# The joint inside the first FFN: band exchange moved from a load to the stores, and another order for the first pair's sums of quarters

## The chip, the core and the metric

The kernel runs on one core of one Trainium2 chip. The metric is device time in microseconds (us) of one execution. Three timed executions of the kernel before gave 2583.55, 2589.14 and 2589.63 us; the median is 2589.14 us.

The engines are named as the profile names them: PE is TensorE (matmuls), PEld its weight loads, DVE is VectorE, ACT is ScalarE, POOL is GpSimd, SP is SyncE, which here only issues transfers. Transfers issued by SP go to the hardware queue that the profile calls q1; transfers issued by POOL, which here add what they read to what already stands in the destination, go to the software queue q0. Both queues are served by the same 16 DMA engines.

## The reference

One layer of a hybrid backbone over 256 latent and 256 context tokens with a model width of 2048: a gated FFN, a mixer (attention and a matrix LSTM side by side), a second gated FFN, a final norm. The change touches only the first FFN, which is done for both sequences, 512 tokens together:

```python
def adaln(x, g, mod, i):
    return rms_norm(x, g) * (1 + mod[:, i + 1, None, :]) + mod[:, i, None, :]

def half_step_ffn(x, mod, i, g, w_up, w_down):
    h = adaln(x, g, mod, i)
    a, b = jnp.split(h @ w_up, 2, axis=-1)
    return x + 0.5 * mod[:, i + 2, None, :] * ((jax.nn.silu(a) * b) @ w_down)
```

`D_FF` is 5632. Everything is float32.

## The kernel before, in words

**Precision.** A float32 operand is kept as two parts, `hi` (rounded) and `lo` (the rest), and a product is three matmuls: hi·hi, lo·hi, hi·lo (`mm3`, L154). The parts of a weight tile are made by `split`: for each half of a 128x2048 tile ACT writes `hi` (L130) and DVE subtracts to get `lo` (L131). There are four buffers for `hi` halves and four for `lo` halves, so the splitting can run about two tiles ahead of PE.

**The gated part, "quads".** The 5632 hidden columns are handled in 11 blocks of 512 (`FB` = 4 columns of 128). Block 0 is made near the start. Blocks 1 to 10 are made by `quad(n)`, each with seven block products instead of eight (a Strassen-like scheme over quarters of tokens and inner dimension). A quad has 14 steps: seven products `m`, two weight tiles `q` each, step number 2m+q. A step is 24 matmuls of 128x512. Some weight tiles are sums of tiles; the sums are made by adding transfers from POOL into a tile that was already used (`accum`, L742), into the two `chain` tiles or into a `raw` tile. At each step the quad also does one item of the modulation products (`mod_items`, loads `sraw` at L239, DVE work at L210).

**Storing a gated block.** A finished quarter of the block (tokens by hidden columns, `ca`) is transposed by DVE in 32x32 squares (L842, in `turned`) and stored to DRAM (L844) as it is. A transposition in 32x32 squares leaves bands of 32 rows in the wrong place. The exchange of these bands is done when the block is loaded again: `hid_load` for n > 0 issues four transfers (L713), each of which gathers rows of 512 B. Block 0 is stored in its final layout and is loaded by one plain transfer (L709).

**The down part, "pairs".** `pair(p)`, p from 0 to 4, multiplies two blocks (2p and 2p+1) with their part of `w_down`, again by seven products (`a11 a12 n1 s4 s2 s3 a22`) of two steps each, 14 steps of 24 matmuls. Each block stands in a tile `raws[0]` or `raws[1]` of 1 MB, which the trace calls `hidh` and `hidl` after the slots they take over. `raws[0]` holds the quarters a11 and a21, `raws[1]` holds a12 and a22. The seven moving operands are sums and differences of these quarters, made in place: v = a22 - a21; n1 = v; v2 = -v - a11 (this is s2); u turns a12 into s4; u2 turns a21 into a11 - a21 (this is s3). DVE makes the differences (L1020, L1021), and `split_to` (ACT L722, DVE L723) puts each operand's hi and lo parts into its place in `sums` (`sumshh` holds a11 a12 n1 s4, `sumshl` holds s2 s3 a22). The first pair takes a11 and a12 from two extra places (`place0`), which are filled in steps 11 and 12 of the last quad. PE's results are copied into `acc` by ACT (L1092) or added to it by DVE (L1094).

**The joint.** In the last quad (`last_steps`) the two blocks of the first pair are loaded at steps 6 and 8. In the first pair everything that a later pair does ahead of time still has to be done. What is done at which step is written in a table, `first_plan` (L1049): each step's words are carried out after that step's weight tile was split. `raw0` and `raw1` there are the loads of the next pair's two blocks (`hid_load` 2 and 3) into the same two places, which is possible once all sums from the place have been made.

**Order of instructions.** The program text gives a priority; a planner with its own estimate of durations makes a fixed list for each engine and queue from it. So an instruction may stand in its engine's list a little earlier or later than its text, and at run time each engine and SP's queue follow their list strictly.

Of the kernel before, what the change touches and what calls it, by code (L numbers as in the profile page):

```python
# [9 lines left out]
F32 = mybir.dt.float32  # L10
# [9 lines left out]
P = 128  # L20
# [8 lines left out]
NF = D_FF // P  # L29
# [18 lines left out]
FB = 4  # L48
CB = 512
# [11 lines left out]
def tile_layer(ctx: ExitStack, tc: tile.TileContext, I: dict, out: bass.AP):  # L61
    nc = tc.nc
# [7 lines left out]
    dr = ctx.enter_context(pool(name="dr", bufs=1, space=DRAM))  # L70
# [4 lines left out]
    def bank():  # L75
        return ps["mm"].tile([P, 512], F32, tag="mm", name="mm")

    def tbank():
        return ps["tr"].tile([P, 512], F32, tag="tr", name="tr")
# [189 lines left out]
    class Beside:  # L269
# [26 lines left out]
        def one(self):  # L296
            i, kt, h = self.items[self.n]
            x, limit = self.slots[self.n]
            mod_half(x, {LAT: self.cB}, None, i, (LAT,), kt, h)
            self.due.append((self.done + 1, self.n))  # L300
            self.n += 1
# [162 lines left out]
    with pool(name="st", bufs=1) as st:  # L464
# [53 lines left out]
        def factor(ss4):  # L518
            s1 = sm.tile([P, 1], F32, tag="s1", name="s1")
            vector[0].tensor_reduce(s1, ss4, axis=AX.X, op=ALU.add)  # L520
            r = sm.tile([P, 16], F32, tag="rstd", name="rstd", bufs=4)[:, :1]
            vector[0].tensor_scalar(r, s1, 1.0 / D, EPS, op0=ALU.mult, op1=ALU.add)
            nc.gpsimd.tensor_tensor(r, r, mhalf[:, :1], op=ALU.pow)
            return r
# [34 lines left out]
        def mod_unit():  # L559
            if ready:  # L560
                return ready.pop(0)
            raw = st.tile([P, 2048], F32, tag="mraw", name="mraw", bufs=4)
            tc.keep_in_program_order(nc.sync.dma_start(raw, I["w_m0"][next(unit)]))
            return raw
# [40 lines left out]
        for s in (CTX, LAT):  # L605
            for t in range(2):
                x = xs0[s, t] = st.tile([P, D], F32, name=f"xs{s}{t}")
# [20 lines left out]
        r = factor(ss)  # L628
        for n, (s, t) in enumerate(((CTX, 1), (LAT, 0), (LAT, 1))):
# [5 lines left out]
            last, r = r, factor(ss)  # L635
# [14 lines left out]
        for k0, k1 in BLOCKS[1:]:  # L650
            kk = slice(k0, k1)
            following = products(1, pre, k0, k1, hhi, hlo, middle=True)
            if k1 - k0 == 2:
                raw = mod_unit()
# [38 lines left out]
        vector[0], tensor[0] = nc.vector, nc.tensor  # L693


    hidd = [dr.tile([4, P, CB] if n else [P, 16, P], F32, name=f"hid{n}") for n in range(NF // FB)]
    NB = NF // FB
    fmcm = pool(name="fm", bufs=1, side="right")
    fm = fmcm.__enter__()
# [3 lines left out]
    def form(tag, name):  # L703
        sp = ft if tag == "t" else fm
        return [sp.tile([P, 2, 8, P], F32R, tag=f"{tag}{x}", name=f"{name}{x}") for x in "hl"]

    def hid_load(n, raw):
        if not n:
            nc.sync.dma_start(raw, hidd[0].rearrange("p m x -> p (m x)"))  # L709
            return  # L710
        rows = hidd[n].rearrange("m (a r) (b x) -> b r (m a) x", a=4, b=4)
        for b in range(4):
            nc.sync.dma_start(raw[32 * b : 32 * b + 32].rearrange("r (m x) -> r m x", x=P), rows[b])  # L713

    def pinned(ins):
        tc.keep_in_program_order(ins)
# [26 lines left out]
    with pool(name="f1u", bufs=1) as f1u:  # L743
# [28 lines left out]
        for f in range(NPRE, FB):  # L772
            pab = []
            for ab in range(2):
                wt = load_split(I["w_up1"][f - NPRE, ab])
                b = bank()
# [6 lines left out]
        n1, s2, s4 = form("n", "n1"), form("s", "s2"), form("t", "s4")  # L783
# [3 lines left out]
        a11, a12, a21, a22 = quarter(0, 0), quarter(0, 1), quarter(1, 0), quarter(1, 1)  # L787
        s3 = a21
# [46 lines left out]
        def turned():  # L835

            if not turn:
                return
            n, t, ca, spare = turn.pop(0)
            if (n, t) == (NB - 1, 3):  # L840
                spare = chp.tile([P, CB], F32, tag="stg", name="stg")
            pinned(nc.vector.transpose(spare, ca))  # L842
            s, tt = divmod(t, 2)
            nc.sync.dma_start(hidd[n][2 * tt + s], spare)  # L844

        add = lambda o, x, y: nc.vector.tensor_tensor(o, x, y, op=ALU.add)
        negative = lambda o, y: nc.vector.scalar_tensor_tensor(o, o, -1.0, y, op0=ALU.mult, op1=ALU.mult)
# [4 lines left out]
        def quad(n, after=lambda step: None):  # L852
# [84 lines left out]
            for m, (a, src, dst, fresh, then, use) in enumerate(order):  # L937
                if fresh:
                    dst.update({s: bank() for s in range(2)})
                for q in range(2):  # L940
                    wt = split(src(q))
                    if then:
                        then(q)
                    after(2 * m + q)
                    for s in range(2):
                        for j in range(4):
                            k = 4 * q + j
                            hi, lo = a[0][:, s, k, :], a[1][:, s, k, :]
                            mm3(dst[s], hi, lo, *wt(slice(j * CB, (j + 1) * CB)), fresh and k == 0, k == 7, True)
                        if q and use:  # L950
                            use(s)
                        elif not s:
                            turned()
# [20 lines left out]
        def last_steps(step):  # L974

            if step not in (6, 7, 8, 9):
                steps(side)
            if step == 6:
                raws.extend(hid_slot("n"))
            if step in (6, 8):  # L980
                hid_load(step // 2 - 3, raws[step // 2 - 3].bitcast(F32))
            if step == 10:
                place0.extend(x.rearrange("p (a c) -> p a c", a=2) for x in hid_slot("s"))
            if step in (11, 12):
                split_to(place0[step - 11], quarters(raws[step - 11].bitcast(F32))[0])
# [7 lines left out]
        while turn:  # L993
            turned()
# [51 lines left out]
        "last1": lambda: last_split(1),  # L1046
    }

    first_plan = {0: "v n1", 1: "v2 u s4", 2: "s2 u2", 3: "s3 a22", 4: "raw0 raw1", 7: "a11", 8: "a12", 9: "v n1", 10: "v2 u", 11: "s4", 12: "s2 u2", 13: "s3"}  # L1049
    plan = {0: "a22 raw0", 1: "raw1", 4: "a11", 5: "a12", 6: "v", 7: "n1", 8: "v2 u", 9: "s4", 11: "s2 u2", 13: "s3"}  # L1050
    last_plan = {0: "a22 raw0", 4: "last0", 5: "last1"}

# [24 lines left out]
    def pair(p):  # L1077
# [80 lines left out]
        for m, (g, src, dst, fresh, then, use) in enumerate(order):  # L1158
            a = place0[m] if p == 0 and m < 2 else place[g]
            for c in range(2):  # L1160
                wt = split(src(c))
                if then:
                    then(c)
                added()
                for x in todo.get(2 * m + c, "").split():
                    if x.startswith("raw"):
                        hid_load(2 * p + 2 + int(x[3]), raws[int(x[3])])
                    else:
                        make[x]()
                if p == NP - 1:  # L1170
                    if (2 * m + c) in GATES:
                        ahead.append(both_gates(GATES[2 * m + c]))
                    if 2 * m + c == 13:
                        last_gate(0)
                        last_gate(1)
                    if m in (1, 4, 6):
                        gates = used[c] = ahead.pop(0)
                    elif m == 5:
                        gates = used[c]
                for s in range(2):  # L1180
                    if fresh:
                        dst[c, s] = tbank() if c and dst is not X else bank()
                    for j in range(FB):
                        k = slice((2 * j + s) * P, (2 * j + s + 1) * P)
                        mm3(dst[c, s], a[:, 0, k], a[:, 1, k], *wt(slice(j * CB, (j + 1) * CB)), fresh and j == 0, j == FB - 1, True)
                    use(c, s)
# [92 lines left out]
    with ExitStack() as mx:  # L1279
# [47 lines left out]
        u = one([P, 4, 2, NH], "u")  # L1327
# [149 lines left out]
        for h in range(NH):  # L1477
            b = bank()
# [82 lines left out]
        for h in range(NH):  # L1561
            b = bank()[:, :T]
# [389 lines left out]
    with f2x:  # L1952
# [28 lines left out]
        for f in range(NPRE, FB):  # L1981
            pab = []
            for ab in range(2):
                wt = load_split(I["w_up2"][f - NPRE, ab])
                b = (tbank() if f == FB - 1 else bank())[:, :T]
# [33 lines left out]
        a11, a12, a21, a22 = quarter(0, 0), quarter(0, 1), quarter(1, 0), quarter(1, 1)  # L2019
        forms2 = {g: f3.tile([P, 2, 8, P], F32R, tag=f"f{i}", name=f"{g}f") for i, g in enumerate(("n1", "s4", "s2", "s3"))}  # L2020
        n1, s4, s2, s3 = ([x[:, 0], x[:, 1]] for x in (forms2[g] for g in ("n1", "s4", "s2", "s3")))
# [263 lines left out]
        for x in sequence():  # L2285
            next(streams[x])
            if x == "u":
                steps(forms)
            clock[0] += 1
            turned()  # L2290
# [164 lines left out]
```

## Time and profile before

| What | Value |
|---|---|
| median of three timed executions | 2589.14 us |
| profiled execution, its own time | 2593.71 us |
| span of the profiled execution | 2592.0 us |
| PE busy | 2557.9 us (99%) |
| DVE busy | 2223.8 us (86%) |
| ACT busy | 1403.2 us (54%) |
| the first FFN's last quad, from step 10 on | from 899.88 us |
| the first pair's first matmul | 924.93 us |

Times in the trace are counted from the start of the span. A row of the timeline has the start, the duration, the engine, the line of the kernel, the operation, the tiles written and read, and in square brackets how long the engine had been idle before and what ended that. Rows marked SPq are transfers being issued; their duration is the time SP spent on issuing. A row of the table by stretches gives, for each engine, busy time and number of instructions, then the granted clock of PE (1.00 is full), the share of the DMA engines' time and GB/s.

### The profile page before, as it was taken

How to read it: one execution, taken by the hardware profiler on the slowest of the kernel's cores; microseconds unless marked ns; L12 is line 12 of the kernel's file. 1: busy time of each engine (PE TensorE's matmuls, PEld its weight loads, DVE VectorE, ACT ScalarE, POOL GpSimd, SP SyncE). 2: the span in 40 equal slices, each digit the busy share in tenths (PEclk: the TensorE clock that was granted, in tenths of full speed). 3: DMA queues.
4: the chain of work that ended last, by engine and by line, in shares of the span. 5: the costliest groups of instructions: out<-in, count | busy, mean ns of one | idle time of the engine just before them, and what ended most of it. 6: DMA issues, size and time to landing. Idle time of an engine off the chain costs nothing. (4 is left out here: it accounts for less than half of the span.)

```text
span 2592.0 us, 33866 instructions
## 1 busy us (share of the span) xinstructions
PE 2557.9 (99%) x12486; PEld 2123.5 (82%) x12486; DVE 2223.8 (86%) x2942; ACT 1403.2 (54%) x1798; POOL 213.8 (8%) x262
## 2 busy tenths in 40 slices
PE   8999999999999999999999999999999999999998
PEld 5788888888887878888889889888898888888886
DVE  7789889888888878888887889898889888898887
ACT  5454444444444455444454347466476676666663
POOL 0000000000000000010110000120000000000001
PEclk8999999999999999999999999999999999999999
DMA  9988999999999999999987887776768999999986
GB/s 392 353 215 260 267 269 268 240 272 270 274 263 271 239 233 237 224 215 232 231 243 265 305 304 249 239 272 220 265 238 241 274 275 277 282 283 274 272 250 169
DMA packets 152182, 675.26 MB, mean 261 GB/s; under 512 B 22728, under 2 KB 43720, under 8 KB 91856
## 3 DMA queue, kind: packets, MB, share of 16 engines
q1 hardware_dynamic: 123936, 490.64, 51.7%
q0 software_dynamic: 28080, 182.46, 35.7%
q8 instruction: 98, 1.61, 0.2%
q14 instruction: 68, 0.56, 0.1%
HBM read 655.15 MB, written 17.89 MB: 260 GB/s over the span
## 5 line engine op out<-in xcount | busy, mean ns | idle before, releaser
L130 ACT ACTIVATE hi<-raw 128x1024 fp32r<-128x1024 f32 (+2 forms) x488 | 503.9, 1039 | 392.8 <-PE mm L154 286.0
L131 DVE TENSOR_TENSOR lo<-raw,hi 128x1024 fp32r<-128x1024 f32 (+2 forms) x476 | 567.4, 1204 | 103.9 <-ACT hi L130 86.4
L130 ACT ACTIVATE hi<-chain 128x1024 fp32r<-128x1024 f32 x352 | 369.0, 1059 | 340.6 <-PE mm L154 183.6
L131 DVE TENSOR_TENSOR lo<-chain,hi 128x1024 fp32r<-128x1024 f32 x352 | 424.5, 1219 | 100.3 <-ACT hi L130 92.8
L154 PE MATMUL mm<-lo,hhi 128*128 128x512 f32 (+3 forms) x1024 | 387.1, 378 | 3.5 <-DVE lo L131 3.4
L154 PE MATMUL mm<-hi,hhi 128*128 128x512 f32 (+3 forms) x1024 | 390.1, 381 | 0.1
L154 PE MATMUL mm<-hi,hlo 128*128 128x512 f32 (+3 forms) x1024 | 386.1, 377 | 0.0
L210 DVE SCALAR_TENSOR_TENSOR junk<-sraw,cBh 128x1024 fp8e5<-128x1024 f32 x192 | 234.2, 1220 | 21.6 <-DMA sraw<-in_w_mt 20.2
L154 PEld LDWEIGHTS mm<-lo,hhi 128*128 128x128 f32 x1024 | 192.4, 188 | 38.8 <-DVE lo L131 6.0
L154 PEld LDWEIGHTS mm<-hi,hhi 128*128 128x128 f32 x1024 | 192.5, 188 | 32.5 <-ACT hi L130 0.8
L154 PEld LDWEIGHTS mm<-hi,hlo 128*128 128x128 f32 x1024 | 192.6, 188 | 31.8
L131 DVE TENSOR_TENSOR lo<-ra,hi 128x1024 fp32r<-128x1024 f32 x104 | 126.0, 1222 | 26.2 <-ACT hi L130 22.6
L130 ACT ACTIVATE hi<-ra 128x1024 fp32r<-128x1024 f32 x104 | 109.7, 1061 | 65.6 <-PE mm L154 34.2
L154 PE MATMUL mm<-lo,hid2h 128*128 128x512 f32 x352 | 137.1, 390 | 0.0
L154 PE MATMUL mm<-hi,hid2h 128*128 128x512 f32 x352 | 137.1, 389 | 0.0
L154 PE MATMUL mm<-hi,hid2l 128*128 128x512 f32 x352 | 137.0, 389 | 0.0
L154 PE MATMUL mm<-hi,sumshl 128*128 128x512 f32 x400 | 123.2, 389 | 0.0
L210 DVE SCALAR_TENSOR_TENSOR sr<-sr,cBl 128x1024 f32<-128x1024 f32 x84 | 102.2, 1224 | 13.5 <-DMA sr<-in_w_mt 6.8
L154 PE MATMUL mm<-hi,sumshh 128*128 128x512 f32 x352 | 108.9, 391 | 0.2 <-DVE acc L1094 0.2
L742 POOL DMA_DIRECT2D chain<-in_w_up1b x51 | 45.1, 885 | 734.4 <-DVE lo L131 586.7
L154 PE MATMUL mm<-hhi,hi 128*128 128x512 f32 (+1 forms) x288 | 101.4, 352 | 0.0
L154 PE MATMUL mm<-hhi,lo 128*128 128x512 f32 (+1 forms) x288 | 99.0, 344 | 0.0
(491 smaller groups left out, 5439.5 us busy)
## 6 DMA issues: line engine op xcount, KB each, us to landing
raw<-in_w_dn SPq DMA_DIRECT2D x70, 1024.0 KB, 10.1
chain<-in_w_up1b POOLq DMA_DIRECT2D x51, 1024.0 KB, 10.5
sraw<-in_w_mt SPq DMA_DIRECT2D x96, 512.0 KB, 7.5
sr<-in_w_mt SPq DMA_DIRECT2D x81, 512.0 KB, 5.7
raw<-in_w_up1b SPq DMA_DIRECT2D x40, 1024.0 KB, 9.5
mraw<-in_w_m SPq DMA_DIRECT2D x32, 1024.0 KB, 7.3
chain<-in_w_dn POOLq DMA_DIRECT2D x30, 1024.0 KB, 10.3
chain<-in_w_up2b POOLq DMA_DIRECT2D x28, 1024.0 KB, 11.2
```

What stands on the lines that cost most here:

```text
L130: scalar[0].activation(hi, src, AF.Copy)
L131: vector[0].tensor_tensor(lo, src, hi.bitcast(F32), op=ALU.subtract)
L154: tensor[0].matmul(out_ap, s, m, start=first and not n, stop=last and n == 2, skip_group_check=skip)
L210: ins = nc.vector.scalar_tensor_tensor(junk() if junk else raw, raw, 1.0, cB[s], op0=ALU.mult, op1=ALU.mult, accum_out=mT[:, i, s, kt, h : ...
L742: accum = lambda dst, src: nc.gpsimd.dma_start(dst, src, accum_op=ALU.add)
```

## The change

1. Block 1 gets the layout of block 0 in DRAM. Its band exchange is done in the stores: each of the quad's four quarters is stored by four transfers of 32 partitions (runs of 512 B) instead of one of 128 partitions (runs of 2 KB). The load of block 1 becomes one plain transfer of 1 MB.
2. In the first pair the sums are made in another order over the steps, and the two places are loaded again at steps 3 and 5 instead of both at step 4. What the next pair needs (a11, a12, v, n1, ...) moves by about a step.

```diff
-    hidd = [dr.tile([4, P, CB] if n else [P, 16, P], F32, name=f"hid{n}") for n in range(NF // FB)]
+    hidd = [dr.tile([4, P, CB] if n > 1 else [P, 16, P], F32, name=f"hid{n}") for n in range(NF // FB)]
...
     def hid_load(n, raw):
-        if not n:
-            nc.sync.dma_start(raw, hidd[0].rearrange("p m x -> p (m x)"))
+        if n < 2:
+            nc.sync.dma_start(raw, hidd[n].rearrange("p m x -> p (m x)"))
             return
...
             pinned(nc.vector.transpose(spare, ca))
             s, tt = divmod(t, 2)
-            nc.sync.dma_start(hidd[n][2 * tt + s], spare)
+            if n > 1:
+                nc.sync.dma_start(hidd[n][2 * tt + s], spare)
+                return
+            rows = hidd[n].rearrange("(b r) m x -> m r b x", b=4)
+            for a in range(4):
+                nc.sync.dma_start(rows[8 * tt + 4 * s + a], spare[32 * a : 32 * a + 32].rearrange("r (b x) -> r b x", b=4))
...
-    first_plan = {0: "v n1", 1: "v2 u s4", 2: "s2 u2", 3: "s3 a22", 4: "raw0 raw1", 7: "a11", 8: "a12", 9: "v n1", 10: "v2 u", 11: "s4", 12: "s2 u2", 13: "s3"}
+    first_plan = {0: "v n1", 1: "v2 u", 2: "u2 s4", 3: "s3 raw0", 4: "s2", 5: "a22 raw1", 8: "a11", 9: "a12", 10: "v n1", 11: "v2 u", 12: "s4 s2", 13: "u2 s3"}
```

## The prediction

> **What bounds the kernel now.** I read the page first, then the busy time by stretches around the joint, then PE's timeline there, then what its waits go back to.
>
> ```profile
> span 2592.0 us, 33866 instructions
> PE 2557.9 (99%) x12486; PEld 2123.5 (82%) x12486; DVE 2223.8 (86%) x2942; ACT 1403.2 (54%) x1798; POOL 213.8 (8%) x262
> ...
> 880.00:920.00 40.00, 37.36 (x164) 30.23 (x163) 26.10 (x36) 16.09 (x17) 2.64 (x3) 1.00 1.02 268
> 920.00:960.00 40.00, 37.11 (x153) 29.00 (x152) 34.92 (x39) 23.35 (x28) 3.53 (x4) 0.96 0.85 206
> 1000.00:1040.00 40.00, 40.00 (x178) 33.15 (x177) 34.24 (x38) 19.39 (x20) 4.42 (x5) 1.00 0.98 240
> ```
>
> PE sets the time, so only what makes PE wait counts. In a steady stretch it is busy 40.00 of 40 us; at the joint it falls to 37.36 and 37.11, and the clock to 0.96. That is all the change can win, and its size comes from the matmuls that open a step:
>
> ```profile
> 899.88 0.39 PE L154 MATMUL mm<-hi,hhi 128*128 128x512 f32 x1
> 905.32 0.39 PE L154 MATMUL mm<-hi,hhi 128*128 128x512 f32 x1
> 911.65 0.50 PE L154 MATMUL mm<-lo,hhi 128*128 128x512 f32 x1 [0.28 <-DVE lo L131]
> 915.67 0.50 PE L154 MATMUL mm<-lo,hhi 128*128 128x512 f32 x1 [2.36 <-DVE lo L131]
> 924.93 0.62 PE L154 MATMUL mm<-hi,hidh 128*128 128x512 f32 x2
> 932.82 0.50 PE L154 MATMUL mm<-lo,hidh 128*128 128x512 f32 x1 [0.48 <-DVE lo L131]
> 948.00 1.25 PE L154 MATMUL mm<-hi,sumshh 128*128 128x512 f32 x4 [0.17 <-DVE acc L1094]
> 951.49 1.92 PE L154 MATMUL tr<-hi,sumshh 128*128 128x512 f32 x4 [2.24 <-DVE acc L1094]
> 974.08 0.62 PE L154 MATMUL mm<-hi,sumshl 128*128 128x512 f32 x2
> ...
> 950.00:952.00 2.00, 0.51 (x2) 0.39 (x3) 2.00 (x4) 1.19 (x2) 0.00 (x0) 0.91 0.62 183
> 952.00:954.00 2.00, 2.00 (x6) 1.40 (x5) 2.00 (x2) 0.00 (x0) 0.00 (x0) 0.50 1.21 221
> 954.00:956.00 2.00, 2.00 (x8) 1.55 (x8) 2.00 (x3) 0.00 (x0) 0.88 (x1) 0.74 1.23 216
> ```
>
> Steps 10 and 11 of the last quad start at 899.88 and 905.32: an undisturbed step takes 5.44 us, four take 21.76. The pair's first matmul comes at 924.93, 25.05 us after step 10: **3.29 us lost**. Its step 4 starts at 948.00, 23.07 later: **1.31 lost**. Its step 8 starts at 974.08, 26.08 later: **4.32 lost**, of which the clock takes 2 x (0.09 + 0.50 + 0.26) = 1.70. Together 8.92 us, 0.34% of the run. Below, T0 is the pair's first matmul (924.93 before), and pair times are counted from it.
>
> **Part 1: the load of block 1.** First the cause of the first loss.
>
> ```profile
> 884.05 18.64 SPq L713 DMA_DIRECT2D hidl<-hid  x1
> ...
> hidh<-hid SPq DMA_DIRECT2D x1, 1024.0 KB, 29.8
> ...
> q0 software_dynamic: 333, 2.47, 98.7%
> q1 hardware_dynamic: 333, 0.16, 6.8%
> ...
> 908.33 1.06 ACT L722 ACTIVATE hidh<-hidh 128x1024 fp32r<-128x1024 f32 x1 [7.41 <-DMA hidh<-hid]
> ...
> 914.39 1.22 DVE L131 TENSOR_TENSOR lo<-chain,hi 128x1024 fp32r<-128x1024 f32 x1
> ```
>
> The two queue rows are the stretch 890 to 902: the queues alternate packet for packet, 333 each, though one moves 2.47 MB and the other 0.16. So a small packet costs q1 a whole turn of q0, 12 x 16 / 333 = 0.58 us. A quarter of block 1 (256 KB in 512 B) is 512 packets, 32 turns on each engine, 18.5 us; one stands ahead of block 0's 1 MB, which lands after 29.8 us. ACT waits 7.41 us for it with the next step's hi halves behind, DVE's lo half comes at 914.39, PE stands until 915.67. SP is held 18.64 us, and the modulation loads behind it then crowd DVE.
>
> After: both blocks are 1 MB in 8 KB packets, 16 turns. An 8 KB packet takes about 0.33 us (the best slice below, 392 GB/s over 16 engines), so 16 x 0.91 = 15 us from about 880: landed near 895, before ACT's turn at 900.9. Q0's adding transfers get up to 16 x 0.33 = 5 us later in exchange, which I hold to be inside the two tiles that the splitting runs ahead. The first loss goes: -3.29 (0 if those transfers then come late). The second is the same delay passed on (the `chain` tile, freed late, is loaded late): -1.31 (bound 0).
>
> ```profile
> GB/s 392 353 215 260 267 269 268 240 272 270 274 263 271 239 233 237 224 215 232 231 243 265 305 304 249 239 272 220 265 238 241 274 275 277 282 283 274 272 250 169
> ...
> DMA packets 3338, 1.66 MB, mean 208 GB/s; under 512 B 95, under 2 KB 3338, under 8 KB 3338
> ```
>
> The second row is 950 to 958, when q1 had the engines alone with 512 B packets: 208 GB/s. [...]
>
> **Part 1: the stores.**
>
> ```profile
> L844 SPq DMA_DIRECT2D hid<-c x20: 326/327/1811, 209.3 to 923.3; - x20
> ...
> 200.00:260.00 60.00, 60.00 (x267) 49.67 (x266) 54.96 (x70) 27.66 (x31) 3.53 (x4) 1.00 0.86 261
> ```
>
> Twelve more issues at 0.327 us are 3.9 us of SP's time, in the stretch 209 to 242. Behind each stand the next quad's `raw` and `chain` loads and `sraw`. A store's 32 turns instead of 8 hold them up to 24 x 0.58 = 14 us where q0 is busy throughout. The cover is the splitting ahead: PE is busy 60.00 of 60 us there. I take 0; the bound is one wait like the one at 915.67, +2.4.
>
> **Part 2: the order of the sums.**
>
> ```profile
> 927.19 2.01 ACT L130 ACTIVATE hi<-chain 128x1024 fp32r<-128x1024 f32 x2 [1.56 <-DMA chain<-in_w_dn]
> ...
> 935.61 1.23 DVE L1020 TENSOR_TENSOR v<-hidl,hidh 128x1024 f32<-128x1024 f32 x1 [1.71 <-issue]
> 943.77 1.22 DVE L723 TENSOR_TENSOR sumshl<-v,sumshl 128x1024 fp32r<-128x1024 f32 x1
> 949.53 1.22 DVE L723 TENSOR_TENSOR sumshl<-hidl,sumshl 128x1024 fp32r<-128x1024 f32 x1
> 951.86 4.62 DVE L131 TENSOR_TENSOR lo<-chain,hi 128x1024 fp32r<-128x1024 f32 x4
> ```
>
> From v at 935.61 (T0 + 10.7) DVE works without a gap to 951.86, where the lo halves of step 4 begin: 16.25 us for 12 wide instructions (4.62/4 = 1.15 each) and 4 additions. That is the third loss: PE wants the first lo half 0.91 us (four matmuls) into step 4, at T0 + 22.7, and has it at 953.0, T0 + 28.1. The new table takes two wide instructions, the lo parts of s2 (943.77) and a22 (949.53), behind those halves: -2.3 us. And v starts earlier, up to 1.6, since the wait of 1.56 us on ACT (927.19) delays the last silu, its store, and so v's memory. So step 4's lo halves begin at T0 + 9.1 + 13.9 = 23.0, the first ends at 24.1, 1.4 late instead of a stall that also drops the clock: **-4.32 becomes +1.3**, so -3.0 (bounds 0 and -4.32).
>
> **Part 2: the second place's reload.** This is what I expect to come late next.
>
> ```profile
> 951.65 4.15 SPq L713 DMA_DIRECT2D hidl<-hid  x4
> ...
> 954.86 0.88 POOL L742 DMA_DIRECT2D chain<-in_w_dn  x1 [20.56 <-DVE lo L131]
> 976.78 0.88 POOL L742 DMA_DIRECT2D chain<-in_w_dn  x1 [4.57 <-DVE lo L131]
> ...
> q0 software_dynamic: 440, 3.21, 96.4%
> q1 hardware_dynamic: 437, 0.22, 6.8%
> ...
> 980.09 1.06 ACT L722 ACTIVATE sumshh<-hidl 128x1024 fp32r<-128x1024 f32 x1 [4.48 <-DMA hidl<-hid]
> ...
> 982.98 1.22 DVE L131 TENSOR_TENSOR lo<-raw,hi 128x1024 fp32r<-128x1024 f32 x1
> ```
>
> Blocks 2 and 3 keep the gathering load: 2048 packets of 512 B each, 128 per engine. Before, both were issued (951.65 the second) when q0 was idle; the six adding transfers of steps 4 to 9 (954.86 to 976.78) reached the engines about 3 us after their issue, at 958, and by then most of both blocks was through. Even so the rest crept (960 to 976: 437 packets beside 440), and ACT waited 4.48 us until 980.09, T0 + 55.2. It cost PE little because PE itself was 4.3 us late.
>
> After, the second reload comes after a22, which comes after four lo halves and s2: 23.0 + 6 x 1.15 = T0 + 29.9. The first adding transfer goes out with step 4's second lo half, T0 + 25.9, and is on the engines at 29. The order is reversed: all 128 packets per engine stand beside q0's train. The train is 6 x 8 packets at 16 x 16 / 440 = 0.58 us, or 5.44 each where PE paces it: it ends near T0 + 60. About 50 of the 128 packets go in its turns, the other 78 at the free rate (3338 in 7.2 us is 29 per engine and us) in 2.7; with 2 for the landing, **T0 + 65**, ten later than before. What it feeds moved by only one step.
>
> What is behind it: ACT's a12 and DVE's v, each with the next tile's halves queued after them. Before, the lo half that PE needed next began 2.9 us after the landing (982.98) and ended at +4.1; so here T0 + 69.1. Which step that is depends on the planner's list. Before, a12 is written at step 8 and stands behind step 9's hi halves; shifted alike, it stands behind step 10's, and step 11 waits. PE reaches step 11 at 59.9 + 1.3 = T0 + 61.2 and wants the lo half at 62.1: **+7.0**, and a clock drop like the one at 952, **+1.7**. Bounds: nothing (a12 placed later still) and +12.4 + 1.7 (a12 ahead of step 10's halves).
>
> **The sum.** -3.29 - 1.31 - 3.0 + 0 + 8.7 = +1.1 us. The profiled execution took 2593.71 us, 4.6 above the median of the three runs; from the median 2589.14 that gives **2590.2 us**: no change that can be told.
>
> **The rivals.**
>
> *The reload isn't decisive.* It is issued ahead of the train, or what it feeds stands late enough in the lists. Then -7.6, 2581.5; at best all 8.92, 2580.2. For it: before, a 4.48 us wait of ACT passed with hardly a wait of PE. Against it: the packet counts of 960 to 976.
>
> *Slower: a12 and v stand ahead of step 10's halves.* The lo half at T0 + 69.1 is wanted at 56.7: 12.4 + 1.7; and nine wide sums (10.4 us) follow that DVE must fit in before the next pair, where before it was already without a gap; I add 3. Sum 17.1 - 7.6 = +9.5, 2598.6. It decides from a landing later than about T0 + 60.
>
> *The order isn't done as written.* The lists need not follow the text: before, s2's lo part (943.77) ran ahead of s4's, written a step earlier. If s2 and a22 are still made before step 4's halves, the third loss and the reload stay as they were and only part 1 pays: -4.6, 2584.5.
>
> **How the numbers follow.** My forecast 0.40, reload not decisive 0.24, slower 0.21, order unchanged 0.15. About 0.3% (7.8 us) is what can be told from no change. Faster by more (below 2581.4) is over half of the second case, 0.15; slower by more (above 2596.9) is most of the third and the tail of the first, 0.21; within, 0.64. The likeliest's own range is 2586 to 2595; the range that takes in the others is 2580 to 2600.
>
> **What would show it.** Part 1: one load each into `hidh` and `hidl`, landing in about 15 us; SP not held; no wait of PE between 899 and 925 nor in the pair's steps 0 and 1. Part 2: s2 and a22 behind step 4's lo halves, clock 1.00 there. The reload: its last 512 B packets 60 us or more behind T0, ACT and DVE waiting on `hidl` for over 8 us, PE on lo halves in step 10 or 11. A landing before T0 + 57, or PE unbroken through steps 9 to 13, would prove the forecast wrong towards faster; PE waits in the second quad, with `chain` or `raw` loads late, would prove the stores wrong.

## The result and the profile after

Eight executions of the changed kernel gave 2600.28 us in the median (2596.63 to 2604.10); beside them, on the same chip, the kernel before gave 2590.05 us (2583.55 to 2594.37). The ratio is 1.0039, interval [1.0024, 1.0053]: the change makes the kernel 0.39% **slower**, about 10 us. Forecast was no difference that can be told, 2590.2 us.

Both profiles show where. The joint reaches from the last quad's end through the first pair, 880 to 1100 us. In the table by stretches the number in brackets behind PE's busy time is its matmuls. An undisturbed matmul takes 5.44/24 = 0.2267 us, so what a stretch of 220 us lost is 220 - 0.2267 x (number of matmuls), idle time and half clock together. First the kernel before, then the changed one, with its quads (120 to 880 us) as well:

```profile
120.00:880.00 760.00, 758.35 (x3337) 623.83 (x3337) 678.61 (x859) 359.32 (x404) 60.22 (x68) 1.00 0.91 259
880.00:1100.00 220.00, 214.29 (x931) 174.68 (x930) 176.29 (x196) 111.84 (x121) 18.54 (x21) 0.99 0.94 231
```

```profile
120.00:880.00 760.00, 757.05 (x3327) 621.74 (x3326) 676.36 (x858) 356.76 (x402) 59.43 (x68) 1.00 0.92 258
880.00:1100.00 220.00, 207.08 (x892) 168.22 (x891) 170.52 (x189) 109.34 (x119) 19.16 (x22) 0.97 0.89 222
```

The joint lost 8.9 us before, the prediction's three losses, and loses 17.8 after: 39 matmuls fewer, 8.8 of the 10 us. The quads lost 3.5 and lose 5.8, a difference that a further execution of the changed kernel does not repeat (below).

The timeline of the changed kernel, PE and what it waits for; T0 is again the pair's first matmul. The stores' new lines move what stands behind them down by five: L1025, L1097 and L1099 here are L1020, L1092 and L1094 of the kernel before.

```profile
902.01 0.39 PE L154 MATMUL mm<-hi,hhi 128*128 128x512 f32 x1
924.00 0.61 PE L154 MATMUL mm<-hi,hidh 128*128 128x512 f32 x2
934.90 1.22 DVE L1025 TENSOR_TENSOR v<-hidl,hidh 128x1024 f32<-128x1024 f32 x1 [2.58 <-DMA hid<-cy]
946.79 0.61 PE L154 MATMUL mm<-hi,sumshh 128*128 128x512 f32 x2
947.45 1.22 DVE L131 TENSOR_TENSOR lo<-chain,hi 128x1024 fp32r<-128x1024 f32 x1
954.33 1.22 DVE L723 TENSOR_TENSOR sumshl<-hidl,sumshl 128x1024 fp32r<-128x1024 f32 x1
955.57 22.62 SPq L713 DMA_DIRECT2D hidl<-hid  x4
970.51 1.06 ACT L130 ACTIVATE hi<-chain 128x1024 fp32r<-128x1024 f32 x1 [0.30 <-PE tr L154]
970.54 0.61 PE L154 MATMUL mm<-hi,sumshl 128*128 128x512 f32 x2
989.66 1.06 ACT L722 ACTIVATE sumshh<-hidl 128x1024 fp32r<-128x1024 f32 x1 [17.60 <-DMA hidl<-hid]
990.62 1.99 ACT L130 ACTIVATE hi<-raw 128x1024 fp32r<-128x1024 f32 x2
992.72 1.19 PE L154 MATMUL mm<-hi,sumshl 128*128 128x512 f32 x2 [11.13 <-ACT hi L130]
```

The three losses of before have become small: from the last quad's step 10 to T0 it takes 21.99 us (0.23 lost), from T0 to step 4 22.79 (1.03), from step 4 to step 8 23.75 (1.99). Then a new one: step 10, due two steps of 5.44 us behind step 8's 970.54, at 981.4, starts at 992.72, **11.3 us late**, because ACT makes step 10's hi halves (990.62) only after a12 (989.66), and a12 waits for the second reload. That was issued at 955.57, right behind a22's lo part (954.33), and landed at T0 + 65.7. The stretches in which the granted clock (third value from the end) falls to 0.50 and comes back give the time between:

```profile
984.00:986.00 2.00, 0.00 (x0) 0.00 (x0) 0.00 (x0) 0.00 (x0) 0.00 (x0) 0.68 1.00 243
...
998.00:1000.00 2.00, 2.00 (x9) 1.60 (x9) 2.00 (x3) 2.00 (x4) 0.00 (x0) 0.91 0.75 315
```

The shares give half speed from 984.7 to 998.4; PE works through the last 5.6 us of it, which costs 2.8 us more.

Why the reload takes 34 us from issue to landing is in the DMA queues. The first pair of rows is 966 to 982 us, while the adding transfers run, the second 985 to 988, when they have ended (packets, MB, share of the engines):

```profile
q0 software_dynamic: 443, 3.24, 97.1%
q1 hardware_dynamic: 443, 0.22, 6.7%
...
q1 hardware_dynamic: 1221, 0.60, 102.8%
q0 software_dynamic: 8, 0.02, 2.7%
```

One packet of 512 B for one adding packet of 8 KB, 443 to 443, in 16 us; once q0 is empty, 1221 small packets go in 3 us.

### The profile page after: what moved, and what is told of

Read it like the earlier page. It is cut to its first block, busy times and chain, and to the rows that moved or that the text cites. A ratio compares the mean times of both kernels' runs of the same rounds, so it can differ in the third digit from the quotient of the medians.

```text
span 2602.4 us, 33873 instructions
## 1 busy us (share of the span) xinstructions
PE 2559.6 (98%) x12486; PEld 2122.6 (82%) x12486; DVE 2222.7 (85%) x2942; ACT 1402.2 (54%) x1798; POOL 213.6 (8%) x262
## 5 line engine op out<-in xcount | busy, mean ns | idle before, releaser
L131 DVE TENSOR_TENSOR lo<-ra,hi 128x1024 fp32r<-128x1024 f32 x104 | 126.1, 1221 | 26.5 <-ACT hi L130 22.9
L154 PE MATMUL mm<-hi,sumshl 128*128 128x512 f32 x400 | 125.1, 394 | 11.1 <-ACT hi L130 11.1
## 6 DMA issues: line engine op xcount, KB each, us to landing
chain<-in_w_dn POOLq DMA_DIRECT2D x30, 1024.0 KB, 10.2
```

The lines of the kernel that those rows point to most:

```text
L131: vector[0].tensor_tensor(lo, src, hi.bitcast(F32), op=ALU.subtract)
L154: tensor[0].matmul(out_ap, s, m, start=first and not n, stop=last and n == 2, skip_group_check=skip)
```

## The experiments

Three theories stood against each other. **A**: the late reload, 512 B packets beside q0's train, is the whole loss. **B**: the small stores of block 1, or the other lists that they bring about in the quads, cost the time. **C**: the new order of the sums itself puts too much on DVE. The losses in the joint and in the quads are worked out from the rows of stretches as above; ratios are to the kernel before, on the same chip.

### One part alone

Part 1 alone (the changed kernel with the old table):

```diff
-    first_plan = {0: "v n1", 1: "v2 u", 2: "u2 s4", 3: "s3 raw0", 4: "s2", 5: "a22 raw1", 8: "a11", ...}
+    first_plan = {0: "v n1", 1: "v2 u s4", 2: "s2 u2", 3: "s3 a22", 4: "raw0 raw1", 7: "a11", ...}
```

> Part 1 alone: block 1 exchanges bands in its stores, the first pair keeps the old order. Theory A (the late reload of block 3 is the whole loss): both plain loads land before ACT needs them, so the losses of 3.29 and 1.31 us before the pair's step 4 go and nothing takes their place; the third (4.32) stays; about 4.6 us faster than before, no wait of PE above 3 us between the pair's steps 8 and 13. Theory B (the stores and the changed lists in the second to the tenth quad cost the time): slower than before by several us, with PE waits between 200 and 880 us. Theory C (the sums' order on DVE costs it): as A here.

Measured: 2588.96 us, ratio 0.9987 [0.9976, 0.9998].

```profile
880.00:920.00 40.00, 40.00 (x178) 33.06 (x177) 29.41 (x42) 18.18 (x20) 2.63 (x3) 1.00 0.95 277
...
880.00:1100.00 220.00, 216.80 (x944) 177.37 (x943) 179.54 (x199) 114.21 (x122) 18.91 (x22) 0.99 0.94 236
948.10 1.24 PE L154 MATMUL tr<-hi,sumshh 128*128 128x512 f32 x4 [2.25 <-DVE acc L1099]
```

The joint loses 6.0, 2.9 less than before: PE is busy without a gap up to 920 us, where the first loss was, and the third loss stays (DVE is late for step 4, the longest wait 2.25 us). Part 1 alone gains.

Part 2 alone (the new table; block 1 stored and loaded as before):

```diff
-    hidd = [dr.tile([4, P, CB] if n > 1 else [P, 16, P], F32, name=f"hid{n}") for n in range(NF // FB)]
+    hidd = [dr.tile([4, P, CB] if n else [P, 16, P], F32, name=f"hid{n}") for n in range(NF // FB)]
     ...  (hid_load and the stores likewise)
```

> Part 2 alone: the new order and the two reloads apart, block 1 stored and loaded as before. Theory A: the losses of 3.29 and 1.31 us stay, and the block 3 load still lands about 65 us after the pair's first matmul, ACT waits about 17 us for it and PE about 11 in step 10 with some 3 us of lowered clock behind it; slower than before by about 12 us, slower than the changed kernel by 2 to 5. Theory B: no slower than before. Theory C: slower, but with PE's waits on DVE's lo halves spread over steps 10 to 13 and no long wait of ACT on the load.

Measured: 2604.0 us, ratio 1.0043 [1.0028, 1.0058].

```profile
880.00:1100.00 220.00, 204.64 (x884) 165.54 (x882) 168.65 (x187) 108.14 (x118) 18.65 (x22) 0.98 0.89 219
995.41 1.19 PE L154 MATMUL mm<-hi,sumshl 128*128 128x512 f32 x2 [10.11 <-ACT hi L130]
```

The joint loses 19.6, and PE's wait is there (10.11) without any small store of block 1. The loss belongs to part 2; B is out as its cause. That it would be 2 to 5 us slower than the changed kernel did not come in full: it is 1.8 us in the joint and about 1 us by the ratios.

### The reload taken out of the way

If A holds, three ways out should each remove the wait. The first keeps part 2 and changes what is loaded: blocks 2 and 3 are also exchanged in their stores, so that the reloads are plain, in packets of 8 KB.

```diff
-    hidd = [dr.tile([4, P, CB] if n > 1 else [P, 16, P], F32, name=f"hid{n}") for n in range(NF // FB)]
+    hidd = [dr.tile([4, P, CB] if n > 3 else [P, 16, P], F32, name=f"hid{n}") for n in range(NF // FB)]
-        if n < 2:
+        if n < 4:
-            if n > 1:
+            if n > 3:
```

> The changed kernel with blocks 2 and 3 also stored with their bands exchanged, so the two reloads in the first pair are plain 1 MB transfers of 8 KB packets (16 packets per engine instead of 256). Order and steps as in the changed kernel. Theory A: the block 3 load lands within about 15 us of its issue, some 45 to 50 us after the pair's first matmul; ACT's wait of 17.6 us and PE's of 11.1 us go; about 14 us faster than the changed kernel, 4 to 6 faster than before. Theory B: slower than the changed kernel, because there are 24 more store issues in two more quads. Theory C: PE still loses about 10 us in steps 10 to 13.

Measured: 2586.59 us, ratio **0.9974** [0.9963, 0.9985], faster than both kernels.

```profile
120.00:880.00 760.00, 756.03 (x3320) 620.05 (x3319) 675.26 (x856) 355.52 (x401) 59.21 (x67) 1.00 0.92 258
880.00:1100.00 220.00, 218.07 (x959) 179.38 (x958) 181.77 (x201) 116.53 (x126) 19.40 (x22) 1.00 0.94 238
957.13 0.33 SPq L709 DMA_DIRECT2D hidl<-hid  x1
973.51 1.05 ACT L722 ACTIVATE sumshh<-hidl 128x1024 fp32r<-128x1024 f32 x1
...
q0 software_dynamic: 336, 2.49, 82.7%
q1 hardware_dynamic: 144, 1.05, 18.8%
hidl<-hid SPq DMA_DIRECT2D x1, 1024.0 KB, 13.2
```

Issued at the same point and beside the same train, the block is there after 13.2 us: 144 packets of q1 carry 1.05 MB (957 to 972 us), where 443 carried 0.22. A12 (973.51) waits for nothing. The joint loses 2.6, and C is out too: the same order of sums, with the block in time, gives the best joint so far.

The second keeps the changed kernel's transfers and moves what needs the block further back in the table:

```diff
-    first_plan = {..., 5: "a22 raw1", 8: "a11", 9: "a12", 10: "v n1", 11: "v2 u", 12: "s4 s2", 13: "u2 s3"}
+    first_plan = {..., 5: "a22 raw1", 8: "a11", 11: "a12 v", 12: "n1 v2 u", 13: "s4 s2 u2 s3"}
```

> The changed kernel with a12 and v moved to step 11 and the sums behind them to steps 12 and 13; ACT's list now has a12 behind the hi halves of steps 10 and 11. The load itself is the same. Theory A in full (the load is late, and it costs PE because of where a12 stands in ACT's list): the load still lands at about 65 us from the pair's first matmul, but PE's 11 us in step 10 go and at most about 3 us come in steps 12 and 13; 8 to 12 us faster than the changed kernel. If the late load slowed PE in another way (through the DMA engines, the weight loads behind it on SP's queue), PE's loss stays about 10 us. Theory C: PE loses more, since the sums are now crowded into steps 12 and 13.

Measured: 2594.2 us, ratio 1.0003 [0.9994, 1.0013].

```profile
960.00:1000.00 40.00, 35.89 (x150) 28.96 (x149) 22.22 (x23) 19.46 (x24) 2.64 (x3) 0.94 0.89 209
880.00:1100.00 220.00, 213.41 (x922) 174.25 (x922) 175.64 (x195) 112.34 (x121) 18.52 (x21) 0.98 0.91 228
923.35 0.62 PE L154 MATMUL mm<-hi,hidh 128*128 128x512 f32 x2
980.22 1.06 ACT L130 ACTIVATE hi<-raw 128x1024 fp32r<-128x1024 f32 x1 [0.30 <-PE mm L154]
990.89 1.06 ACT L722 ACTIVATE sumshh<-hidl 128x1024 fp32r<-128x1024 f32 x1 [9.61 <-DMA hidl<-hid]
993.43 0.73 PE L154 MATMUL mm<-hi,sumshl 128*128 128x512 f32 x2 [2.14 <-ACT hi L130]
996.13 0.79 PE L154 MATMUL mm<-lo,sumshl 128*128 128x512 f32 x1 [1.97 <-DVE lo L131]
```

The block lands as late as before, T0 + 67.5. But the hi halves of steps 10 and 11 (the last at 980.22) now stand ahead of a12, and PE's two waits are 2.1 and 2.0 us instead of 11.1. The place in the list decides how much of a late landing PE sees. The joint still loses 11.0: besides these 4.1, the clock of 0.94 over the 40 us in which the waits lie is worth up to 2.4, and the rest is step 4's lo halves and what follows, which I did not take apart.

The third puts both reloads ahead of the adding transfers, still gathered in 512 B:

```diff
-    first_plan = {..., 3: "s3 raw0", 4: "s2", 5: "a22 raw1", 8: "a11", ...}
+    first_plan = {..., 3: "s3 a22 raw0 raw1", 4: "s2", 8: "a11", ...}
```

> The changed kernel with a22 and both reloads put back to step 3, ahead of step 4's lo halves (s2 stays behind them); block 3 keeps its gathering load of 512 B packets. Same bytes, same packets, same places of a12 and v in the text; only the reload now goes out some 7 us earlier, ahead of the train of adding transfers. If the train is what it crawls beside, most of the 128 packets per engine pass in front of it, it lands 10 to 25 us earlier than in the changed kernel (40 to 55 us after the pair's first matmul), and PE's 11 us wait goes: 9 to 13 us faster than the changed kernel, about 3 faster than before. If the number of packets is the cause by itself, the landing comes only 7 us earlier and PE still waits 4 to 7 us.

Measured: 2589.65 us, ratio 0.9983 [0.9973, 0.9993].

```profile
880.00:1100.00 220.00, 216.47 (x946) 177.94 (x945) 178.91 (x198) 114.83 (x124) 19.41 (x22) 0.99 0.94 234
949.63 2.44 SPq L713 DMA_DIRECT2D hidl<-hid  x4
951.36 0.80 PE L154 MATMUL mm<-lo,sumshh 128*128 128x512 f32 x1 [3.10 <-DVE lo L131]
```

Six microseconds earlier at issue, and the long wait is gone without any other layout. A12 (975.75) waits for nothing. The block lands sooner than the 40 to 55 us that were expected: between 860 and 1030 us transfers into this place took 7.5 us from issue to landing in the median and 14.5 at most (31.4 in the median for this block in the changed kernel). The last of the four was issued before 952.1, which gives an estimate of T0 + 35, and T0 + 42 at the latest. In exchange a22 is again made ahead of step 4's halves, and PE waits 3.1 us for them: the third loss is back. The joint loses 5.5.

### How the two queues share

The changed kernel with half of the second reload: two of the four bands of block 3 are loaded.

```diff
-        for b in range(4):
+        for b in range(2 if n == 3 else 4):
```

> The changed kernel, but the reload of block 3 brings only its first two bands (64 of 128 partitions, 1024 packets of 512 B instead of 2048); the other half of the block is left out, so what is computed from it is not the reference's. One turn for one turn: of 64 packets per engine some 44 to 50 go while the train of adding transfers lasts, the rest right behind it, so the landing comes only 2 to 3 us earlier than the changed kernel's T0 + 65.7, at about T0 + 63, and PE still waits 8 to 9 us (time about 3 us below the changed kernel). If the two queues shared the engines by bytes or in proportion to the work that stands in them, half the bytes would land in about half the 34 us from the issue, near T0 + 48, PE would not wait, and the time would be about 13 us below the changed kernel.

Beside it, on the same chip, the changed kernel once more:

> The changed kernel once more, as it is. Shows which of its losses are in every execution: the wait of PE of 11.1 us near step 10 of the pair should be there again within 1.5 us. The 3 us that PE lost in the quads between 400 and 500 us of its first profile should be gone or elsewhere if they vary by execution, and there again if the small stores of block 1 made them.

The half reload:

```profile
880.00:1100.00 220.00, 209.55 (x908) 170.96 (x907) 172.46 (x192) 109.68 (x120) 18.50 (x21) 0.98 0.89 223
q0 software_dynamic: 441, 3.22, 96.6%
q1 hardware_dynamic: 442, 0.22, 6.7%
...
922.81 0.62 PE L154 MATMUL mm<-hi,hidh 128*128 128x512 f32 x2
985.17 1.06 ACT L722 ACTIVATE sumshh<-hidl 128x1024 fp32r<-128x1024 f32 x1 [14.59 <-DMA hidl<-hid]
988.23 1.19 PE L154 MATMUL mm<-hi,sumshl 128*128 128x512 f32 x2 [8.13 <-ACT hi L130]
```

The changed kernel again:

```profile
120.00:880.00 760.00, 758.01 (x3340) 624.57 (x3339) 678.40 (x860) 358.45 (x404) 60.09 (x68) 1.00 0.92 259
880.00:1100.00 220.00, 206.28 (x894) 167.49 (x893) 170.77 (x190) 108.68 (x119) 18.50 (x21) 0.98 0.89 222
991.32 1.19 PE L154 MATMUL mm<-hi,sumshl 128*128 128x512 f32 x2 [10.98 <-ACT hi L130]
```

The two queue rows are again 966 to 982 us. With half the packets waiting in q1, they go at the same pace as before, 442 beside 441 of the train. The half block lands at T0 + 62.4, 3 us earlier and not 17, and PE still waits 8.13 us: a turn for a turn, with 64 packets per engine to load as with 128. The two single executions took 2596.55 and 2604.30 us; of these 7.8 us the joints account for about 3 (14.2 against 17.3), and the rest lies elsewhere. In the repeat the wait is there again (10.98), but the quads lose 2.8 where the first profile had 5.8: that part varies from execution to execution.

### The stores, and the best version

The small stores in all ten blocks that the quads make (conditions `n > 10`, `n < 11`):

> All of blocks 1 to 10 exchange their bands in the stores and are loaded by one plain transfer each; the order of the changed kernel. If the gathering loads cost PE only where they meet the adding transfers in the first pair, this is the same as the kernel with blocks 1 to 3 so stored (2586.6) within 2 us, and the 160 store issues are hidden. If the exchanging stores, eight of whose packets replace two, cost PE by themselves, it is slower than that kernel by 3 us or more, with new waits of PE before 880 us.

Measured: 2593.96 us, ratio 0.9998 [0.9988, 1.0007], by the ratios 6 us above the version with three blocks.

```profile
120.00:880.00 760.00, 752.30 (x3297) 617.43 (x3297) 671.27 (x851) 352.94 (x398) 58.31 (x66) 1.00 0.93 257
880.00:1100.00 220.00, 218.63 (x964) 180.39 (x963) 183.47 (x204) 116.64 (x125) 20.27 (x23) 1.00 0.91 239
```

The joint is the best of all (1.5), but the quads lose 12.6, above the 2.8 to 7.4 of the kernels shown here. So the stores do cost when every quad makes them. Whether SP's issues, the small packets or the lists do it was not separated.

Three blocks in the stores, with the old table (the `first_plan` of the kernel before):

> Blocks 1 to 3 exchange bands in their stores as before it, but the first pair keeps the old order of the sums. It measures the new order by itself where no reload is late. If two wide DVE instructions fewer ahead of step 4's lo halves are worth what the prediction said, PE loses 4 to 5 us around 950 (clock drop included) instead of 2, and this is about 3 us slower than with the new order, 2589 to 2590. If the order is worth nothing once the loads are quick, the two are equal within 1 us.

Measured: 2589.54 us, ratio 0.9988 [0.9975, 1.0000].

```profile
880.00:1100.00 220.00, 217.48 (x950) 178.21 (x948) 180.66 (x199) 116.13 (x124) 18.91 (x22) 0.99 0.93 237
```

Its joint loses 4.6, the new table's 2.6: 2 us of worth for the new order once the reload is plain. The medians, 2589.54 and 2586.59, point the same way with overlapping intervals.

Blocks 1 and 3 in the stores, block 2 gathered as in the changed kernel:

```diff
-    hidd = [dr.tile([4, P, CB] if n > 3 else [P, 16, P], F32, name=f"hid{n}") for n in range(NF // FB)]
+    hidd = [dr.tile([4, P, CB] if n > 3 or n == 2 else [P, 16, P], F32, name=f"hid{n}") for n in range(NF // FB)]
     ...  (hid_load and the stores likewise)
```

> Blocks 1 and 3 exchange their bands in the stores and are loaded plainly; block 2 keeps the plain stores and the gathering load of 512 B, at step 3, ahead of the adding transfers of steps 4 to 9. If only the load that stands beside the train of adding transfers matters, the joint loses about 3 us as with blocks 1 to 3, and the time is within 2 us of 2586.6 (with a quarter less... that is 12 fewer small stores, at best 1 us better). If any gathering load in the joint is harmful, block 2's still lands late: it holds SP as block 3's did and block 3's plain load behind it waits, ACT waits 5 us or more for hidl, and the time is nearer 2594.

Measured: 2586.59 us, ratio **0.9979** [0.9970, 0.9988].

```profile
880.00:1100.00 220.00, 218.74 (x963) 180.19 (x962) 182.53 (x203) 116.93 (x127) 19.42 (x22) 1.00 0.95 241
943.77 1.93 SPq L713 DMA_DIRECT2D hidh<-hid  x4
```

The gathering load at 943.77, ahead of the train, does no harm: the joint loses 1.7. So of the two gathering loads only the one that stood beside the train mattered. This version and the one with three blocks are equal, both faster than the kernel before by 5 to 7 us.

## Why the prediction was wrong

What came is the prediction's rival "slower: a12 and v stand ahead of step 10's halves", which it gave 2598.6 us and a chance of 0.21. Point by point:

**The step that failed** is the sentence "shifted alike, it stands behind step 10's, and step 11 waits". The words moved by a step in the table, a12 from step 8 to step 9, but not in ACT's list: a12 stands right behind step 9's hi halves (970.51), as it did before. So step 10 waited, a step earlier than forecast, and for its hi halves, which ACT makes, not only for the lo. The forecast had +7.0 and 1.7; the trace has 11.3 and 2.8, which is 5.4 of the 9.1 us between the forecast +1.1 and the +10.2 that were timed. Of the others, 1.9 are old losses that stayed, 0.5 is what is left in the joint, and 1.3 lie outside it. The version with the sums later shows the other half of that sentence: behind the halves of steps 10 and 11, the same landing costs PE 4.1 us of waits.

**The reload** was right in its mechanism and its time: the forecast landing was T0 + 65, the measured one is T0 + 65.7, and the half reload bears out the turn for a turn (442 packets beside 441). Closer up, from 970 to 970.66 us, a little over one turn of 16 x 16 / 443 = 0.58 us, the 16 engines moved 16 packets of each queue in the changed kernel. The train was to end near T0 + 60; from 985, T0 + 61, q0 moves hardly anything (8 packets up to 988). The free rate, 1221 packets in 3 us or 25 per engine and us, is a little under the 29 taken. The 2 us that the sum adds for the landing no run shows: the last small packets go between 989.2 and 989.4, and ACT begins a12 at 989.66.

**Part 1, the load** was right in kind: one transfer each, ACT not waiting for `hidh`, the first loss down from 3.29 to 0.23. The landing was mis-sized: the load of `hidh` took 20.3 us from its issue at 880.59, not 15, which was still in time for ACT at 903.10. The second loss was taken to go with the first, -1.31; it went down by 0.28 only. With part 1 alone it stayed: there the pair's first matmul comes at 921.51 and step 4 at 944.62, 23.11 us later, 1.35 lost. So it was not the same delay passed on; what causes it stays open. Part 1 by itself measured 2.9 us in the joint, where the sum had 4.6.

**Part 1, the stores** at 0 holds for one block as far as the quads show it: they lose 2.8 in the repeat and 3.5 in the kernel before. It doesn't hold for ten blocks.

**Part 2, the order** did what it says: s2's and a22's lo parts ran behind step 4's lo halves, which began at T0 + 23.45 (forecast 23.0). The third loss fell to 1.99 (forecast 1.3). That the two times are so near is partly luck. V began at T0 + 10.9, not up to 1.6 us earlier as forecast: it waits 2.58 us, by the profile for the last quarter's store. From v to the halves DVE has 12.55 us of work instead of 16.25: two wide instructions fewer, as forecast, and also two additions to `acc` fewer, 1.2 us together, which now come behind the first half (948.59 and 951.46).

**The rival's price** was 12.4 + 1.7 + 3 - 7.6 = +9.5. By the trace it is 11.3 + 2.8 + 0.5 (what is left of the joint's 17.8) - 5.7 (what the three old losses gave) = +8.9, and +10.2 was timed. The 3 us for DVE falling behind did not come, and the old losses gave back 1.9 less than thought; that these two errors nearly cancel is luck.

## What to carry to other kernels

Here a load of many small packets beside a train of large ones on another queue went on by one packet for each of the train's (443 to 443 in 16 us); what helped was fewer and larger packets (13.2 us from issue to landing instead of 34), or an issue ahead of the train (PE's longest wait 3.10 us instead of 11.13), and half the packets helped little (3 us), since they were still more than the train's (64 per engine to 711 / 16 = 44 from 958 to 984.5). Moving a word in a plan by a step need not move the instruction in its engine's list by a step: the place of the instruction that will wait has to be read from the list, since what stands behind it sets the loss. And when several waits at a joint are removed one by one, ask for each part what it makes late next: here a part that gains 3 us alone and a part that loses 11 alone were one change, and with a plain reload the second part gains too.

## What the runs showed of the hardware

The price of a clock drop was not the same in two executions of the changed kernel. After idle spells of PE of 11.13 and 10.98 us, the half clock lasted 13.7 us in the first profile and 10.2 us in the repeat, and PE worked 5.6 us and 3.1 us of it, at a loss of 2.8 and 1.6 us. The repeat's rows for its two ends:

```profile
984.00:986.00 2.00, 0.00 (x0) 0.00 (x0) 0.00 (x0) 0.00 (x0) 0.00 (x0) 0.55 1.21 229
994.00:996.00 2.00, 2.00 (x10) 1.59 (x9) 1.77 (x3) 0.79 (x1) 0.00 (x0) 0.89 0.37 74
```

The shares give 984.2 to 994.4 there, against 984.7 to 998.4. What set the two lengths was not shown.
